# Keys of dilated attention stored in the order of their tokens' residues modulo 4, and a fourth key buffer in place of two slots

## The chip, the core and the metric

The kernel runs on one core of one Trainium2 chip. The metric is the device time of one execution in microseconds; of a kernel with several runs the median is given. Engines are named TensorE (PE, with its weight loads PEld), VectorE (DVE), ScalarE (ACT) and SyncE (SP, which issues all loads and stores here); GpSimd has no part in it.

## What is computed

Two layers work on a sequence of 1024 tokens of width 1024 in float32. In each layer the normalised input is projected to four heads of a gated linear recurrence and to eight attention heads of width 64; both outputs are projected back, and a squared-ReLU layer of width 4096 follows. The attention is causal and has three patterns whose outputs are merged by their softmax denominators: a window of 128 with step 1, of 512 with step 4, of 2048 with step 16.

```python
DILATED_PATTERNS = ((128, 1), (512, 4), (2048, 16))
...
    for window, dilation in DILATED_PATTERNS:
        o, lse = dilated_window_attention(q, k, v, window, dilation)
        outs.append(o)
        lses.append(lse)
    weights = jax.nn.softmax(jnp.stack(lses, axis=0), axis=0)
    o = jnp.einsum('pbhs,pbhsd->bhsd', weights, jnp.stack(outs, axis=0))
```

A key is seen by a query of pattern (window, d) only if both tokens have the same residue modulo d. Steps 4 and 16 both keep the residue modulo 4.

## The kernel before

Every function only records operations (`op`, with engines, an assumed cost, what it reads and writes). `Program.order` then simulates the engines with those costs and writes one fixed order for each engine; `weave` mixes two generators, so that attention stands among projections. Buffers come from pools of the sizes in `COUNT` (line 38): `slot` is a tile of 128 x 512 float32 (71 of them), `kk` one of 128 x 1024 (3), `sc` a bank of PSUM for scores (2). An operation is placed only when its pool has room, so the sizes of the pools change the order too. An engine works strictly in its order; SyncE's order is that of the DMA issues, and an issue that waits holds up those behind it.

Precise products are made of float32r parts: a tile is split in a high and a low part (`split`, `hilo`: a cast on ScalarE, line 323, and a subtraction on VectorE, line 325).

`attn_proj` makes queries and keys of four heads at a time. For j = 1 (keys) the two halves of the rotation come out of two subtractions and additions (lines 828 and 829), are split, and are stored to DRAM buffers kh and kl (line 843), each row of a store being 512 tokens of one feature. Queries (j = 0) are also stored in a second order, q4, by residue modulo 4 (lines 848 to 851).

A head loads its keys, 64 rows of 1024 tokens for each half of the rotation, in two tiles of the pool kk: the high part and the low part (`Head.k`, line 903).

Attention runs in units (head, n) with n from 0 to 5. Units 0 to 3 are near blocks: 128 queries against adjoining keys, widths 128, 256, 384, 512, and four times 256. Units 4 and 5 are far blocks: 128 queries of one residue against the 256 keys of that residue, the slice (x, S, 4) (line 927). `scores` makes a block in two products, one for each part of the keys (line 952), in a bank of PSUM; one instruction of VectorE adds the bias tile tpt, writes the result to SBUF and takes the extreme of each row (line 957). ScalarE takes exponentials (line 968), TensorE transposes (lines 1057 and 1102), the transposed probabilities are split, and products with the values follow (lines 1071 and 1115). Half of the units run beside the second key projection (`attn_proj(1)`), half beside the output projection.

In the squared-ReLU stage `norm_up` puts as many of the four pairs b11 in tiles of the pool kk as that pool has (line 1222); the others take two slots each.

Of the kernel before, what the change touches and what calls it, by code (L numbers as in the profile page):

```python
# [11 lines left out]
F32 = mybir.dt.float32  # L12
# [3 lines left out]
OP = mybir.AluOpType  # L16
# [10 lines left out]
W = 512  # L27
# [7 lines left out]
EARLY = 10  # L35


COUNT = {"kk": 3, "slot": 71, "raw": 4, "trig": 2, "whi": 8, "wlo": 8, "ls": 4, "last": 2, "row": 2, "rc": 4, "z": 2, "gemm": 3, "sc": 2, "tr": 2, "acc": 1,
         "dram": 1 << 20, "const": 1 << 20}
LOOKAHEAD = {"PE": 60e3, "SP": 36e3}  # L40
PATIENCE = 5e3
# [213 lines left out]
def trunk(ctx: ExitStack, tc: tile.TileContext, xT, wts, cols, trig, toep, lmask, ident_d, out):  # L255
# [58 lines left out]
    def whole(b):  # L314
        return b, lambda: b.t
# [261 lines left out]
    for l in range(L):  # L577
# [75 lines left out]
        def hgrn_rec(p, pr):  # L653
            for m in range(2):
                h = 2 * p + m
                last = None
                for hf in range(NH):
# [146 lines left out]
                    hout[h][hf] = keep_  # L804
                    yield

        def attn_proj(u):
            grp = [Group(g0 + 8 + 3 * u + j, f"w{l}a{u}{j}") for j in range(3)]
            q4[u] = Buf(f"q4{l}{u}", "dram", [2, 32, 2, 4, W], F32)
            for hf in range(NH):  # L810
# [7 lines left out]
                for j in range(2):  # L818
# [6 lines left out]
                    tt(whole(t3), whole(pa), whole(sn_), OP.mult)  # L825
                    tt(whole(t2), whole(pb), whole(sn_), OP.mult)
                    tt(whole(t4), whole(pb), whole(cs_), OP.mult)
                    tt(whole(t1), whole(t1), whole(t2), OP.subtract)
                    tt(whole(t3), whole(t3), whole(t4), OP.add)

                    if j == 0:
                        qk_st[0, u, hf] = Buf(f"q{l}{u}{hf}", "dram", [2, 32, 2, 4, W], F32)
# [2 lines left out]
                    for o, t in ((0, t1), (1, t3)):  # L835
                        th, tl = hilo(t, "rt")
                        for part, y in enumerate((th, tl)):
                            if j == 0:
                                d = qk_st[0, u, hf]
                                load(d, lambda d=d, o=o, part=part: d[part, :, o], lambda y=y: y.t.bitcast(F32), 1 << 18, y, True)  # L840
                            else:
                                d = qk_st[1, u][part]
                                load(d, lambda d=d, o=o, hf=hf: d[:, o, :, hf * W:(hf + 1) * W], lambda y=y: y.t.bitcast(F32),
                                     1 << 18, y, True)
                        if j == 0 and hf == 1:
                            for part, y in enumerate((th, tl)):
                                z = slot("rp", F32R)
                                op("ACT", c_act(W), [z], [y], lambda e, z=z, y=y: A.copy(
                                    z.t.rearrange("p (r a) -> p r a", r=4), y.t.bitcast(F32).rearrange("p (a r) -> p r a", r=4)))
                                load(q4[u], lambda d=q4[u], o=o, part=part: d[part, :, o], lambda z=z: z.t.bitcast(F32),  # L850
                                     1 << 18, z, True)
# [89 lines left out]
        def scores(hd, n, st, at):  # L941
# [3 lines left out]
            for i, (q, q0, keys, x0) in enumerate(blocks(hd, n)):  # L945
                w = len(range(*keys.indices(S)))
                if t is None or o + w > W:
                    t, ps, o = slot("sp"), bank("sc", "sc"), 0

                def emit(e, ps=ps, q=q, q0=q0, keys=keys, o=o, w=w):  # L950
                    for part, k in enumerate(k2):
                        PE.matmul(ps[:, o:o + w], lhsT=q[:, q0:q0 + 128], rhs=k[:, keys], start=part == 0, stop=part == 1)  # L952

                op("PE", 2 * c_mm(w), [ps], [q] + k2, emit, join=o > 0)

                def emit(e, ps=ps, t=t, o=o, w=w, m=st.part(at + i), x0=x0):
                    V.tensor_tensor_reduce(t[:, o:o + w], ps[:, o:o + w], tpt[:, x0:x0 + w], -0.125, 3e38,  # L957
                                           OP.add, OP.min, m.t)

                op("DVE", c_tt(w), [t, st.part(at + i)], [ps, tpt], emit, join=True)  # L960
                sp.append((t, o, w))
                o += w
# [613 lines left out]
```

## Time and profile before

| what | value |
|---|---|
| median of 3 runs | 2428.82 us (2427.02 to 2429.88) |
| profiled execution | 2435.95 us |
| its span | 2434.2 us |
| TensorE busy | 2390.8 us (98%) |
| VectorE busy | 1733.8 us (71%) |
| ScalarE busy | 1217.5 us (50%) |
| mean granted clock of TensorE | 0.993 |

The span runs from the first to the last instruction of the profiled execution. Busy times are unions of the recorded instructions. A matmul's recorded length includes the pipeline, so that lengths of neighbours overlap; the pace is the distance between starts. In the waits, "A <- B" says that A stood idle until B was done.

### The profile page before, as it was taken

How to read it: one execution, taken by the hardware profiler on the slowest of the kernel's cores; microseconds unless marked ns; L12 is line 12 of the kernel's file. 1: busy time of each engine (PE TensorE's matmuls, PEld its weight loads, DVE VectorE, ACT ScalarE, POOL GpSimd, SP SyncE). 2: the span in 40 equal slices, each digit the busy share in tenths (PEclk: the TensorE clock that was granted, in tenths of full speed). 3: DMA queues.
4: the chain of work that ended last, by engine and by line, in shares of the span. 5: the costliest groups of instructions: out<-in, count | busy, mean ns of one | idle time of the engine just before them, and what ended most of it. 6: DMA issues, size and time to landing. Idle time of an engine off the chain costs nothing.

```text
span 2434.2 us, 35321 instructions
## 1 busy us (share of the span) xinstructions
PE 2390.8 (98%) x12572; PEld 2029.5 (83%) x12572; DVE 1733.8 (71%) x3414; ACT 1217.5 (50%) x2391; POOL 0.2 (0%) x4
## 2 busy tenths in 40 slices
PE   9999999999999999999999999999999999999998
PEld 7888898887888878888888988898878888888887
DVE  6365877778988667765744668677889885786575
ACT  7233346665744554445532433466656455554453
POOL 0000000000000000000000000000000000000000
PEclk9999999999999999999999999999999999999999
DMA  4011365953455469656420114668344653786562
GB/s 177 27 35 53 130 212 174 272 159 122 160 207 195 152 216 317 222 181 226 169 83 18 62 53 150 209 177 267 120 165 147 225 181 138 261 310 224 182 218 94
DMA packets 189681, 407.19 MB, mean 167 GB/s; under 512 B 22656, under 2 KB 25536, under 8 KB 189504
## 3 DMA queue, kind: packets, MB, share of 16 engines
q1 hardware_dynamic: 189504, 404.93, 49.7%
q8 instruction: 99, 1.62, 0.3%
q14 instruction: 78, 0.64, 0.1%
HBM read 291.37 MB, written 113.48 MB: 166 GB/s over the span
## 4 chain that ended last, share of the span: by engine, by line
PE 91%; DMA 4%; DVE 2%; ACT 2%; SPq 0%; issue 0%; DVEq 0%; ACTq 0%
PE psd L1415 8%; PE psd L1416 8%; PE psd L1417 8%; PE psu L1264 8%; PE psu L1265 8%; PE psu L1266 8%; PE sc L952 2%; PE pa L705 2%; PE pso L383 2%; PE pso L382 2%; PE pso L384 2%; PE pv L1115 1%; PE psv L407 1%; PE psq L382 1%; PE psv L408 1%; PE psv L409 1%
## 5 line engine op out<-in xcount | busy, mean ns | idle before, releaser
L325 DVE TENSOR_TENSOR al<-al,ah 128x512 fp32r<-128x512 f32 x224 | 152.7, 686 | 51.3 <-ACT ah L323 50.7
L323 ACT CAST ah<-al 128x512 fp32r<-128x512 f32 x224 | 137.4, 618 | 97.9 <-DMA al<-a 50.9
L968 ACT ACTIVATE sp<-sp,ls 128x256 f32<-128x256 f32 (+2 forms) x192 | 100.0, 523 | 17.7 <-DVE ls L957 17.3
L957 DVE CUSTOM_DVE_ANT_0 sp<-sc,tpt 128x256 f32<-128x256 f32 (+1 forms) x192 | 83.1, 439 | 35.6 <-PE sc L952 34.0
L952 PE MATMUL sc<-k,hd 128*128 128x256 f32 (+3 forms) x384 | 95.0, 358 | 12.7 <-DMA k<-kl 7.2
L952 PEld LDWEIGHTS sc<-k,hd 128*128 128x128 f32 x384 | 61.2, 195 | 19.6 <-DVE ls L957 6.1
L1247 ACT ACTIVATE c<-c 128x512 f32<-128x512 f32 x96 | 60.5, 630 | 33.2 <-DVE c L312 33.0
L323 ACT CAST pth<-ptr 128x512 fp32r<-128x512 f32 (+1 forms) x96 | 51.3, 552 | 39.5 <-PE ptr L1102 38.1
L1248 ACT ACTIVATE c<-c 128x512 f32<-128x512 f32 x108 | 68.4, 633 | 3.4
L325 DVE TENSOR_TENSOR ptl<-ptr,pth 128x512 fp32r<-128x512 f32 (+1 forms) x96 | 60.7, 641 | 10.9 <-ACT pth L323 9.8
L705 PEld LDWEIGHTS pa<-q,k 128*112 128x112 f32 (+3 forms) x512 | 62.0, 184 | 3.4
L705 PE MATMUL pa<-q,k 128*112 128x64 f32 (+3 forms) x512 | 61.2, 262 | 0.0
L312 DVE TENSOR_TENSOR x<-x,psd 128x512 f32<-128x512 f32 (+1 forms) x68 | 41.8, 652 | 25.3 <-PE psd L1417 25.1
L312 DVE TENSOR_TENSOR x<-x,pso 128x512 f32<-128x512 f32 x64 | 43.4, 681 | 15.2 <-PE pso L384 14.7
L1102 PE MATMUL ptr<-ident,sp 128*128 128x128 f32 x352 | 53.3, 276 | 0.5 <-ACT sp L968 0.4
L1264 PE MATMUL psu<-bt3h,s3h 128*128 128x512 f32 x128 | 50.6, 395 | 3.2 <-ACT u L319 3.2
L1122 ACT COPY pvt<-pv 64x256 f32<-64x256 f32 x80 | 29.6, 370 | 47.0 <-PE pv L1115 45.5
L713 DVE COPY_PREDICATED at<-lmt,pa 126x256 f32<-126x256 uint8 (+1 forms) x64 | 32.8, 512 | 25.1 <-PE pa L705 24.4
L1265 PE MATMUL psu<-bt3l,s3h 128*128 128x512 f32 x128 | 50.3, 393 | 0.0
L1266 PE MATMUL psu<-bt3h,s3l 128*128 128x512 f32 x128 | 50.3, 393 | 0.0
L1265 PE MATMUL psu<-bt1l,s1h 128*128 128x512 f32 x128 | 49.8, 389 | 0.0
L1266 PE MATMUL psu<-b22h,s4l 128*128 128x512 f32 x128 | 49.8, 389 | 0.0
(4980 smaller groups left out, 8136.0 us busy)
## 6 DMA issues: line engine op xcount, KB each, us to landing
al<-a SPq DMA_DIRECT2D x96, 256.0 KB
w0u<-in_wts_dram SPq DMA_DIRECT2D x42, 512.0 KB
w1u<-in_wts_dram SPq DMA_DIRECT2D x42, 512.0 KB
a<-c SPq DMA_DIRECT2D x76, 256.0 KB
al<-a0t SPq DMA_DIRECT2D x64, 256.0 KB
al<-a1t SPq DMA_DIRECT2D x64, 256.0 KB
hd<-q SPq DMA_DIRECT2D x48, 256.0 KB
a0t<-t SPq DMA_DIRECT2D x48, 256.0 KB
```

The source lines that it names most:

```text
L312: lambda e: V.tensor_tensor(dst[1](), a[1](), b[1](), op=kind))
L323: op("ACT", c_act(n), [hi[0]], [src[0]], lambda e: A.copy(hi[1](), src[1]()), join=join)
L325: lambda e: V.tensor_tensor(lo[1](), src[1](), hi[1]().bitcast(F32), op=OP.subtract), join=join)
L705: PE.matmul(pa[0:128 - b, c * 64:c * 64 + 64], lhsT=k[:, c * 128:c * 128 + 128 - b], rhs=by_half(q)[:, c, :, 1, :], start=True, stop=True)
L952: PE.matmul(ps[:, o:o + w], lhsT=q[:, q0:q0 + 128], rhs=k[:, keys], start=part == 0, stop=part == 1)
L968: op("ACT", c_act(w) + 190, [t, sum_], [t, m], lambda e, t=t, o=o, w=w, m=m, sum_=sum_: A.activation(t[:, o:o + w], t[:, o:o + w], AF.Exp, ...
L1264: PE.matmul(ps.t, lhsT=wh[:, cs], rhs=xh.t, start=first and k == 0, stop=False, skip_group_check=True)
L1265: PE.matmul(ps.t, lhsT=wh[:, cs], rhs=xl.t, start=False, stop=False, skip_group_check=True)
L1266: PE.matmul(ps.t, lhsT=wl[:, cs], rhs=xh.t, start=False, stop=k == 3, skip_group_check=True)
L1415: PE.matmul(ps.t, lhsT=wh[:, cs], rhs=th.t[:, ts], start=first and j == 0, stop=False, skip_group_check=True)
L1416: PE.matmul(ps.t, lhsT=wh[:, cs], rhs=tl.t[:, ts], start=False, stop=False, skip_group_check=True)
L1417: PE.matmul(ps.t, lhsT=wl[:, cs], rhs=th.t[:, ts], start=False, stop=j == 15, skip_group_check=True)
```

## The change

Keys are written by the rotation in the order of residue modulo 4 first and position in that residue second, 512 tokens as 4 runs of 128. The store puts each of the four runs where the whole sequence's run of that residue is, so that a stored row has four runs of 256 tokens. Far blocks read 256 adjoining keys; near blocks read four runs, their scores lie by residue in PSUM, and VectorE's instruction of line 957 reads them in the order of tokens while bias and output keep their order. The pool kk has 4 tiles instead of 3, the pool of slots 69 instead of 71, which is the same memory, and `norm_up` now puts all four pairs in kk.

```diff
--- before.py
+++ after.py
@@ -35,7 +35,7 @@
 EARLY = 10
 
 
-COUNT = {"kk": 3, "slot": 71, "raw": 4, "trig": 2, "whi": 8, "wlo": 8, "ls": 4, "last": 2, "row": 2, "rc": 4, "z": 2, "gemm": 3, "sc": 2, "tr": 2, "acc": 1,
+COUNT = {"kk": 4, "slot": 69, "raw": 4, "trig": 2, "whi": 8, "wlo": 8, "ls": 4, "last": 2, "row": 2, "rc": 4, "z": 2, "gemm": 3, "sc": 2, "tr": 2, "acc": 1,
          "dram": 1 << 20, "const": 1 << 20}
 LOOKAHEAD = {"PE": 60e3, "SP": 36e3}
 PATIENCE = 5e3
@@ -804,6 +804,12 @@
                     hout[h][hf] = keep_
                     yield
 
+        def tokens(t):
+            return t, lambda: t.t.rearrange("p (a r) -> p a r", r=4)
+
+        def by_residue(t):
+            return t, lambda: t.t.rearrange("p (r a) -> p a r", r=4)
+
         def attn_proj(u):
             grp = [Group(g0 + 8 + 3 * u + j, f"w{l}a{u}{j}") for j in range(3)]
             q4[u] = Buf(f"q4{l}{u}", "dram", [2, 32, 2, 4, W], F32)
@@ -825,8 +831,14 @@
                     tt(whole(t3), whole(pa), whole(sn_), OP.mult)
                     tt(whole(t2), whole(pb), whole(sn_), OP.mult)
                     tt(whole(t4), whole(pb), whole(cs_), OP.mult)
-                    tt(whole(t1), whole(t1), whole(t2), OP.subtract)
-                    tt(whole(t3), whole(t3), whole(t4), OP.add)
+                    if j == 0:
+                        tt(whole(t1), whole(t1), whole(t2), OP.subtract)
+                        tt(whole(t3), whole(t3), whole(t4), OP.add)
+                    else:
+                        k1, k3 = slot("kp"), slot("kp")
+                        tt(by_residue(k1), tokens(t1), tokens(t2), OP.subtract)
+                        tt(by_residue(k3), tokens(t3), tokens(t4), OP.add)
+                        t1, t3 = k1, k3
 
                     if j == 0:
                         qk_st[0, u, hf] = Buf(f"q{l}{u}{hf}", "dram", [2, 32, 2, 4, W], F32)
@@ -840,8 +852,9 @@
                                 load(d, lambda d=d, o=o, part=part: d[part, :, o], lambda y=y: y.t.bitcast(F32), 1 << 18, y, True)
                             else:
                                 d = qk_st[1, u][part]
-                                load(d, lambda d=d, o=o, hf=hf: d[:, o, :, hf * W:(hf + 1) * W], lambda y=y: y.t.bitcast(F32),
-                                     1 << 18, y, True)
+                                load(d, lambda d=d, o=o, hf=hf: d.t.rearrange("i o h (r a) -> i o h r a", r=4)[
+                                    :, o, :, :, hf * 128:hf * 128 + 128], lambda y=y: y.t.bitcast(F32).rearrange(
+                                        "p (r a) -> p r a", r=4), 1 << 18, y, True)
                         if j == 0 and hf == 1:
                             for part, y in enumerate((th, tl)):
                                 z = slot("rp", F32R)
@@ -949,13 +962,21 @@
 
                 def emit(e, ps=ps, q=q, q0=q0, keys=keys, o=o, w=w):
                     for part, k in enumerate(k2):
-                        PE.matmul(ps[:, o:o + w], lhsT=q[:, q0:q0 + 128], rhs=k[:, keys], start=part == 0, stop=part == 1)
+                        dst, src = ps[:, o:o + w], k.t.rearrange("p (r a) -> p r a", r=4)
+                        if keys.step:
+                            src = src[:, keys.start]
+                        else:
+                            src = src[:, :, keys.start // 4:keys.stop // 4]
+                        PE.matmul(dst, lhsT=q[:, q0:q0 + 128], rhs=src, start=part == 0, stop=part == 1)
 
                 op("PE", 2 * c_mm(w), [ps], [q] + k2, emit, join=o > 0)
 
-                def emit(e, ps=ps, t=t, o=o, w=w, m=st.part(at + i), x0=x0):
-                    V.tensor_tensor_reduce(t[:, o:o + w], ps[:, o:o + w], tpt[:, x0:x0 + w], -0.125, 3e38,
-                                           OP.add, OP.min, m.t)
+                def emit(e, ps=ps, t=t, o=o, w=w, m=st.part(at + i), x0=x0, step=keys.step):
+                    s, dst, bias = ps[:, o:o + w], t[:, o:o + w], tpt[:, x0:x0 + w]
+                    if not step:
+                        s = s.rearrange("p (r a) -> p a r", r=4)
+                        dst, bias = (x.rearrange("p (a r) -> p a r", r=4) for x in (dst, bias))
+                    V.tensor_tensor_reduce(dst, s, bias, -0.125, 3e38, OP.add, OP.min, m.t)
 
                 op("DVE", c_tt(w), [t, st.part(at + i)], [ps, tpt], emit, join=True)
                 sp.append((t, o, w))
```

Where instructions move: on SyncE, at the second head of the first layer; kh and kl are the stored parts of keys, k a head's tile. Before:

```order
L344 DMA k<-kh_2398 64x1024 x2
L344 DMA hd<-q_2272 128x512
L344 DMA hd<-q_2590 128x512
L344 DMA mh_3_1_0_3366<-mhh 128x512
L344 DMA mh_3_1_1_3373<-mhl 128x512
L344 DMA hd<-q_2597 128x512
L344 DMA q_3406<-rth 32x4x512 x2
L344 DMA q_3406<-rtl 32x4x512 x2
L344 DMA hd<-q_2272 128x512
L344 DMA k<-kl_2412 64x1024 x2
L344 DMA trig<-in_trig_dram 128x512 x2
```

Now:

```order
L344 DMA k<-kh_2400 64x1024 x2
L344 DMA k<-kl_2414 64x1024 x2
L344 DMA hd<-q_2272 128x512
L344 DMA mh_3_1_0_3376<-mhh 128x512
L344 DMA mh_3_1_1_3390<-mhl 128x512
L344 DMA hd<-q_2592 128x512
L344 DMA hd<-q_2599 128x512
L344 DMA q_3413<-rth 32x4x512 x2
L344 DMA q_3413<-rtl 32x4x512 x2
L344 DMA hd<-q_2272 128x512
L344 DMA k<-kh_2400 64x1024
L344 DMA trig<-in_trig_dram 128x512 x2
```

The load of the low part has moved from behind the loads of queries and the stores to right behind that of the high part; where it stood, the third head's high part begins.

On VectorE, at the rotation of the first keys (t are the rotation's products, kp the new tiles, rth and rtl the parts). Before:

```order
L312 TENSOR_TENSOR t_2363<-psb,trig 128x512
L312 TENSOR_TENSOR t_2369<-psb,trig 128x512
L312 TENSOR_TENSOR t_2311<-t_2311,t_2363 128x512
L312 TENSOR_TENSOR t_2313<-t_2313,t_2369 128x512
L312 TENSOR_TENSOR q<-q,tot 128x4x64
L325 TENSOR_TENSOR rtl<-t_2311,rth 128x512
L325 TENSOR_TENSOR rtl<-t_2313,rth 128x512
```

Now:

```order
L312 TENSOR_TENSOR t_2363<-psb,trig 128x512
L312 TENSOR_TENSOR t_2369<-psb,trig 128x512
L312 TENSOR_TENSOR kp<-t_2311,t_2363 128x128x4
L312 TENSOR_TENSOR kp<-t_2313,t_2369 128x128x4
L312 TENSOR_TENSOR q<-q,tot 128x4x64
L325 TENSOR_TENSOR rtl<-kp,rth 128x512 x2
```

The two last steps of the rotation write four-run tiles of their own instead of writing over an input; what follows keeps its place.

On TensorE, at the end of the first head and the start of the second (line 1102 before is 1123 now, 952 is 970, 1057 is 1078). Before:

```order
L1071 MATMUL pv<-pp,v_3202 128x256
L1071 MATMUL pv<-pp,v_3282 128x256
L1071 MATMUL pv<-pp,v_3211 128x256
L1071 MATMUL pv<-pp,v_3286 128x256
L975 MATMUL lt<-ident,ls 32x128
L952 MATMUL sc<-k,hd 128x128 x2
L952 MATMUL sc<-k,hd 128x384 x2
```

Now:

```order
L1123 MATMUL ptr<-ident,sp 128x128 x4
L970 MATMUL sc<-k,hd 128x256 x2
L970 MATMUL sc<-k,hd 128x128 x2
L382 MATMUL psa<-n_1h,w0a111h 128x512
L383 MATMUL psa<-n_1l,w0a111h 128x512
L384 MATMUL psa<-n_1h,w0a111l 128x512
L382 MATMUL psa<-n_1h,w0a111h 128x512
```

The second head's first score product, 128 columns, stood behind the first head's last value products and now stands among the products of the key projection some 25 rows earlier.

## Rows read from the trace of the kernel before

**Rows 1.** the page, busy us, share of the span and instructions of each engine
```profile
PE 2390.8 (98%) x12572; PEld 2029.5 (83%) x12572; DVE 1733.8 (71%) x3414; ACT 1217.5 (50%) x2391; POOL 0.2 (0%) x4
```

**Rows 2.** stretches: length, PE, PEld, DVE, ACT, POOL busy (count), clock, DMA share, GB/s
```profile
330.00:550.00 220.00, 211.28 (x1319) 187.45 (x1317) 166.39 (x444) 137.59 (x378) 0.00 (x0) 0.99 0.68 206
1534.00:1755.00 221.00, 213.15 (x1321) 188.74 (x1320) 166.67 (x445) 137.82 (x380) 0.00 (x0) 0.98 0.67 205
380.00:430.00 50.00, 49.04 (x334) 45.02 (x333) 40.88 (x109) 34.56 (x91) 0.00 (x0) 1.00 0.57 170
```

**Rows 3.** timeline, TensorE, far products: start us, length, line, operation, tiles, shapes, count
```profile
1598.74 1.09 PE L952 MATMUL sc<-k,hd 128*128 128x256 f32 x4
1599.65 0.42 PE L382 MATMUL psa<-n_1h,w1a111h 128*128 128x512 f32 x1
...
1601.48 0.70 PE L952 MATMUL sc<-k,hd 128*128 128x256 f32 x2
1601.99 0.44 PE L382 MATMUL psa<-n_1h,w1a111h 128*128 128x512 f32 x1
```

**Rows 4.** timeline, TensorE, near products of a later head
```profile
1614.42 0.40 PE L952 MATMUL sc<-k,hd 128*128 128x256 f32 x2
1614.66 0.28 PE L407 MATMUL psva<-w1a121h,n_0h 128*128 128x256 f32 x1
```

**Rows 5.** waits of TensorE, whole run: who for whom, us, times, longest
```profile
PE sc L952 <- DMA k<-kl: 7.2, 7, 2.2
PE pv L1115 <- DVE ar L1124: 4.7, 8, 1.0
PE sc L952 <- DVE ls L957: 4.5, 4, 2.5
```

**Rows 6.** timeline, SyncE's queue, loads and stores around the second head's keys
```profile
368.16 1.12 SPq L344 DMA_DIRECT2D k<-kl  x2
369.38 1.00 SPq L344 DMA_DIRECT2D trig<-in_trig_dram  x2
370.48 0.57 SPq L344 DMA_DIRECT2D kh<-rth  x1
...
373.60 1.33 SPq L344 DMA_DIRECT2D k<-kh  x2
```

**Rows 7.** timeline, TensorE, two waits for the low part of keys
```profile
372.55 0.22 PE L952 MATMUL sc<-k,hd 128*128 128x128 f32 x1
374.04 0.71 PE L952 MATMUL sc<-k,hd 128*128 128x128 f32 x3 [1.26 <-DMA k<-kl]
...
497.28 0.33 PE L952 MATMUL sc<-k,hd 128*128 128x128 f32 x1 [1.89 <-DMA k<-kl]
```

**Rows 8.** stretches after two such waits, granted clock third from the end
```profile
498.40:501.80 3.40, 3.40 (x15) 3.14 (x14) 1.21 (x3) 0.00 (x0) 0.00 (x0) 0.50 1.03 242
1580.40:1583.80 3.40, 3.40 (x13) 2.82 (x12) 1.91 (x8) 2.26 (x8) 0.00 (x0) 0.50 1.05 281
```

**Rows 9.** VectorE by line and shape: count, busy us, mean ns, idle before
```profile
L957 DVE CUSTOM_DVE_ANT_0 sp<-sc,tpt 128x256 f32<-128x256 f32 x144 | 59.2, 416 | 28.6 <-PE sc L952 27.8
L957 DVE CUSTOM_DVE_ANT_0 sp<-sc,tpt 128x128 f32<-128x128 f32 x16 | 4.6, 288 | 4.2 <-PE sc L952 4.1
L687 DVE COPY_PREDICATED at<-lmt,pa 128x128 f32<-128x128 uint8 x32 | 14.1, 441 | 0.3
L312 DVE TENSOR_TENSOR ar<-ar,rb 128x512 f32<-128x512 f32 x24 | 16.5, 685 | 0.8 <-DMA rb<-l 0.4
L312 DVE TENSOR_TENSOR rb<-rb,ar 128x512 f32<-128x512 f32 x4 | 4.3, 1072 | 1.4 <-DMA rb<-l 1.4
```

**Rows 10.** the page, the DMA queue of loads and stores: packets, MB, share
```profile
q1 hardware_dynamic: 189504, 404.93, 49.7%
```

**Rows 11.** waits of all engines, VectorE's for scores
```profile
DVE sp L957 <- PE sc L952: 34.0, 45, 3.5
```

## The prediction

> **What bounds the kernel now.** I read the busy shares first. TensorE is busy for 2390.8 of 2434.2 us [rows 1], so whatever shortens its own work is paid back almost in full, and work of another engine counts only where TensorE waits for it. Then the stretches: the change touches the two attention stages (330 to 550 us and 1534 to 1755 us) and the key projections just before and in them. In the two stages together TensorE is busy 424.4 of 441 us, so it idles 16.6 us, and VectorE is busy 333.1 us, 76% [rows 2]. Third, the timeline of TensorE, for the pace of one score product (a matmul's length overlaps the next one, so the pace is read from start to start). Four products against every fourth key, 256 columns each, run from 1598.74 to 1599.65: 0.228 us each [rows 3]. Two products of the same 256 columns against adjoining keys run from 1614.42 to 1614.66: 0.12 us each [rows 4]. Shape, types and weights are alike; only the step between the keys that are read differs. Last, what TensorE waits for: in the whole run 7.2 us, in 7 waits, for the low part of a head's keys to land, which is the largest entry; then 4.7 us for the sums of attention values and 4.5 us for VectorE to take a bank of scores [rows 5].
>
> **Part 1, far score products (patterns that step by 4).** Per head 4 blocks times 2 parts of the keys; 16 heads in the two layers: 128 products. Their keys become adjoining, and 0.228 becomes 0.12 us: 128 x 0.108 = 13.8 us. Where such a group stands behind transposes it is a little slower still (0.51 us for the two at 1601.48) [rows 3], 0.255 - 0.12 = 0.135 each, and 128 x 0.135 = 17.3 is the other end. I take 14.5, near the group of four, which stands among ordinary work. All of it is TensorE's own time.
>
> **Part 2, near score products.** Their keys are now read as 4 runs of a quarter of the width, 32 to 128 adjoining keys. No row shows a read with three jumps in it. A jump at every key costs 0.108 us for 256 of them, 0.4 ns each; three jumps in each of 256 products would be 0.3 us in all. I take 0; the other end, every near product as slow per column as a far one, is rival 4.
>
> **Part 3, VectorE reads the near scores in another order.** The bank now holds the scores by residue, and the instruction that adds the bias steps by a quarter of the width at every element, to put them back in the order of tokens. Columns: 128 + 256 + 384 + 512 + 4 x 256 = 2304 a head, 36,864 in all; the 64 far instructions stay as they are. No row shows such a read of a PSUM bank by this instruction. The nearest row is the product of two tiles in SBUF, one read at a step of 128 elements: 1072 ns for 512 elements where the same work in order takes 685 [rows 9], 0.756 ns more for each. By that row: 36,864 x 0.756 = 27.9 us of VectorE, the near 256-column instruction going from 416 to about 610 ns. Lower end 0 (a stepped read cannot be quicker than 416 ns, which is already a column a cycle beside the 288 of 128 columns: 1.0 ns each). Upper end, the masked copy that writes every second element, 441 ns for 128 against 288 [rows 9]: 1.2 ns each, 44 us. I take 27.9.
> By the Trainium skill (PSUM — Partial Sum Buffer, Specifications (TRN2)) PSUM has lines of 8 bytes, and a non-contiguous pattern slows matmuls significantly; it gives no figure for VectorE, and no run here shows one. If it holds for VectorE's reads, every element of these fetches a line of its own, which speaks for a price at least like that of the SBUF row and for rival 3.
>
> What hides it: in the two stages VectorE has 441 - 333 = 108 us free. After the change it has 333 + 28 + 3 (part 4) = 364 us of work beside 424 - 14.5 = 410 us of TensorE's, 89%. A stretch that already runs so, 380 to 430 us, has VectorE at 40.9 of 50 us, 82%, with TensorE idle for only 0.96 us [rows 2]: a high share alone doesn't stop TensorE. But the score banks are two, so a longer read gives a bank back later, by 0.19 us for 256 columns and 0.39 for 512; behind it on VectorE stand the low parts of the transposed probabilities, for which the value products wait. TensorE's two waits on VectorE, 4.7 + 4.5 = 9.2 us now, grow; I let them grow by half, +5 us. Ends: 0 (all covered) and +28 (all on the path).
>
> **Part 4, the keys' rotation writes by residue.** 16 instructions of 512 elements that now write at a step of 128: by the same row 16 x 0.387 = 6.2 us of VectorE, half of it in the attention stages, half in the stage before, where it stands under products of the projection. On the path 0; if the cover were gone, 6. Two more slots are held for a moment, and the pool has two fewer; no slot wait is among TensorE's large entries [rows 5], so 0, with 3 us as the price if the shorter pool delays a load or a transpose now and then.
>
> **Part 5, stores of the keys in runs of 512 bytes.** 32 stores, 128 rows each, three more packets a row: 12,288 more. The queue's mean packet takes 49.7% x 2434 x 16 / 189,504 = 0.102 us [rows 10]; if each added one took as long (they are a fourth of the size), a group of four stores would take 1536 x 0.102 / 16 = 9.8 us more of the transfer engines; if time goes by bytes, 0. Such a group stands on SyncE's queue right behind the loads of trigonometric tables at 369 us, and keys of the next head are the loads behind it. I take 0 on the path, because with part 6 these keys are wanted a head later, some 27 us; without that cover a part of the 9.8 would stand in front of a head, in four places.
>
> **Part 6, the fourth buffer.** With three, a head's high part is loaded early, and its low part only when the head before has done its last far product: issued at 368.16 [rows 6], wanted at 372.6, arrived at 374.04, 1.26 us late; at 497.28 it is 1.89 us late [rows 7]. With four, both parts stand together on SyncE's queue, a head ahead, so the 7.2 us of [rows 5] go. After the two longest of these waits the granted clock is 0.5, its lower level, for 3.4 us (498.4 and 1580.4) [rows 8]; at half pace 1.7 us are lost each time, 3.4 in both. What is late next: the transfers are not idle (share 0.68 and 0.67 in the stages [rows 2]), so the value loads or a merge's small transfers may end a wait that is covered by the key wait today. Ends: -10.6 and 0. I take -8.
>
> **Sum.** -14.5 - 8 + 5 = -17.5 us. The profiled execution took 2435.95 us, 1.75 around its span; it would take 2418.5. The median of the runs is 2428.82, 7.1 below the profiled one, and the terms are absolute, so 2428.8 - 17.5 = 2411.3; I write 2412.
>
> **Rivals.**
> 1. The forecast, with VectorE's price near the SBUF row: 2412, by the terms' usual spread 2403 to 2421. Chance 0.55.
> 2. Stepped reads of PSUM are free: VectorE gets no longer (but for part 4) and the +5 goes, 2407. For it: nothing in the trace shows a stepped PSUM read. Against it: 1072 against 685 in SBUF. Chance 0.14. The Trainium skill (VectorE: DVE Perf Modes, Mode 1× (REGULAR) — the baseline) says that the plain mode makes no assumption on strides or PSUM operands and gives a result a cycle; by that rule this rival would hold, but the SBUF row, at nearly 2 ns an element, does not agree with it.
> 3. VectorE becomes the bound, and the kernel is slower. Place: the near scores in both stages. It decides from (410 - 333 - 3) / 36,864 = 2.0 ns more an element, nearly three times the SBUF row. At 3.0 ns VectorE has 333 + 3 + 111 = 447 us of work, already above today's 441 for the stages with no idle time; VectorE's present waits for scores, 34 us [rows 11], don't all go, and with a third of them left the stages take 458: 2428.8 + 17 = 2446. For it: the unknown price in PSUM. Against it: both measured prices of stepping are 0.76 and 1.2. Chance 0.10.
> 4. The change doesn't do what it says: the slow pace of far products isn't the step of the keys, or four-run reads are as slow. Then part 1 gives nothing, and -8 + 5 remain: 2426. Against it: 0.12 beside 0.228 with nothing else different. Chance 0.07.
> 5. Waits come back: part 1 holds, but the queues are written for a VectorE that keeps up, the waits on it double (+10), and the keys' 8 us turn up as waits for values or for the merge: 2428.8 - 14.5 + 10 = 2424. For it: TensorE already waits for the sums of values. Chance 0.14.
>
> **How the numbers follow.** A measurement of this kernel can tell some 0.2%, 4.9 us, from no change: faster is below 2424, slower above 2433.7. Faster: cases 1, 2 and half of 5, 0.76; slower: case 3, 0.10; the same: case 4 and the other half of 5, 0.14. The range: low end, all of parts 1 and 6 at their better ends with no price in part 3, 2428.8 - 17.3 - 10.6 = 2401; high end 2426, which takes in case 5 and leaves out case 3 and part of case 4.
>
> **What would show it.** Far products at 0.12 us from start to start; near ones unchanged. The bias instruction of 256 columns in two groups, 416 ns for far and about 610 for near; the rotation's two at about 1.07 us. No wait of TensorE for keys, and no clock at 0.5 near the start of a head. TensorE's waits for VectorE at 12 to 16 us instead of 9. The forecast is wrong if near products slow down, if the bias instruction takes over 0.9 us for 256 columns, or if TensorE's idle time in the stages grows above today's 16.6 us.

## The result, and the profile after

The changed kernel takes 2409.42 us (median of 4 runs, 2408.74 to 2411.52) beside 2427.92 for the kernel before on the same chip (4 runs, 2420.86 to 2429.88): ratio 0.9923 [0.991, 0.9935], 18.5 us less. The forecast was 2412, 2401 to 2426. The profiled run took 2409.73 us, of which 2407.9 are the span. The profile of before was taken from a run of 2435.95 us, some 7 above its median, so differences between these two profiles are too large by about as much; a second profile of before, below, corrects for that.

The page after, busy us, share of the span and instructions, and then its row on the DMA queue (packets, MB, share of 16 engines' span):

```profile
PE 2370.5 (98%) x12572; PEld 2014.9 (84%) x12572; DVE 1734.8 (72%) x3414; ACT 1216.5 (51%) x2391; POOL 0.2 (0%) x4
...
q1 hardware_dynamic: 201792, 404.93, 50.3%
```

TensorE is busy 20.3 us less than in [rows 1] with the same 12,572 instructions; a part of that is chance, since the stretches at the lower clock sum to 36.6 us in that profile and 21.0 in this one, and the means of several profiles, below, give 16.3. VectorE, which was to get longer by 34 us, is busy 1.0 us more. The queue has the 12,288 packets more that the prediction counted on top of [rows 10], and its share rose by 0.6 points.

TensorE's timeline, far products (start, length, line, operation, count), with the instruction behind each group:

```profile
1582.40 0.65 PE L970 MATMUL sc<-k,hd 128*128 128x256 f32 x4
1582.88 0.44 PE L382 MATMUL psa<-n_1h,w1a111h 128*128 128x512 f32 x1
...
1600.27 0.40 PE L970 MATMUL sc<-k,hd 128*128 128x256 f32 x2
1600.51 0.28 PE L407 MATMUL psva<-w1a120h,n_0h 128*128 128x256 f32 x1
```

The four far products take 0.48 us from their start to the start of the next instruction, 0.12 each, where [rows 3] has 0.228. The two near ones in the last pair of lines, now read in four runs, take 0.24, as in [rows 4].

VectorE by form (line, operation, shapes, count | busy us, mean ns | idle before and its releaser):

```profile
L979 DVE CUSTOM_DVE_ANT_0 sp<-sc,tpt 128x256 f32<-128x256 f32 x144 | 58.4, 415 | 23.3 <-PE sc L970 22.3 <-issue 0.2
...
L312 DVE TENSOR_TENSOR kp<-t,t 128x512 f32<-128x512 f32 x16 | 17.1, 1086 | 0.0
...
L979 DVE CUSTOM_DVE_ANT_0 sp<-sc,tpt 128x512 f32<-128x512 f32 x16 | 10.9, 681 | 0.1
```

and the last of them in the kernel before:

```profile
L957 DVE CUSTOM_DVE_ANT_0 sp<-sc,tpt 128x512 f32<-128x512 f32 x16 | 11.0, 684 | 2.3 <-PE sc L952 2.1
```

Line 979 is the 957 of [rows 9]. Its 144 instructions of 256 columns, 80 of which now step through PSUM, take 415 ns where all took 416, and the widest ones, all stepped, take 681 where they took 684. A stepped read of PSUM costs VectorE nothing here. The rotation's write to `kp`, stepped in SBUF, takes 1086 ns, as the prediction priced it from 1072.

What TensorE waits for, whole run (us, times, longest):

```profile
PE pso L382 <- ACT ma_0h L323: 4.9, 2, 2.5
PE sc L970 <- DVE ls L979: 4.9, 10, 1.1
PE ptr L1123 <- ACT sp L989: 4.2, 4, 1.8
PE sc L970 <- DMA hd<-q: 3.0, 3, 1.8
...
PE pv L1136 <- DVE ar L1145: 0.6, 2, 0.3
```

No wait for keys is left of the 7.2 us of [rows 5], and the wait of the value products for the attention sums fell with it, from 4.7 to 0.6. In their place stand waits of score products for queries (`hd`), 3.0 us, and of transposes for ScalarE's exponentials, 4.2. Only the second comes in every profile: the three runs below that keep this order of instructions and fast far products wait for queries 0.3 us or not at all, and for exponentials 6.0 to 7.6.

SyncE's queue, where [rows 6] has the low part of the keys late:

```profile
345.23 1.09 SPq L344 DMA_DIRECT2D k<-kh  x2
346.37 1.24 SPq L344 DMA_DIRECT2D k<-kl  x2
```

Both parts are asked for together, at 345 us, for the second head, whose first score products run at 368.30.

The attention stages, and the stretch behind one of the new waits (length, PE, PEld, DVE, ACT, POOL busy, granted clock, DMA share, GB/s):

```profile
331.00:541.00 210.00, 203.59 (x1327) 181.75 (x1326) 168.28 (x450) 139.34 (x381) 0.00 (x0) 1.00 0.70 216
1520.00:1731.00 211.00, 204.17 (x1326) 182.64 (x1325) 168.58 (x450) 138.78 (x381) 0.00 (x0) 0.99 0.70 215
...
1661.90:1665.30 3.40, 3.40 (x13) 2.88 (x11) 1.25 (x3) 0.71 (x2) 0.00 (x0) 0.50 1.06 339
```

The stages' 441 us of [rows 2] are 421 now, and TensorE's idle time in them went from 16.6 to 13.2 us. The last line shows that the clock still falls: behind a wait of 1.84 us for queries, at 1661.02, the granted clock is 0.50 for 3.4 us, the lower of its two levels (1.2 of 2.4 GHz), while TensorE is busy throughout.

### The profile page after: what moved, and what is told of

Read it like the earlier page. It is cut to its first block, busy times and chain, and to the rows that moved or that the text cites. A ratio compares the mean times of both kernels' runs of the same rounds, so it can differ in the third digit from the quotient of the medians.

```text
span 2407.9 us, 35355 instructions
## 1 busy us (share of the span) xinstructions
PE 2370.5 (98%) x12572; PEld 2014.9 (84%) x12572; DVE 1734.8 (72%) x3414; ACT 1216.5 (51%) x2391; POOL 0.2 (0%) x4
## 4 chain that ended last, share of the span: by engine, by line
PE 91%; DMA 3%; DVE 2%; ACT 2%; issue 1%; SPq 0%; DVEq 0%; ACTq 0%
PE psd L1438 8%; PE psd L1437 8%; PE psd L1436 8%; PE psu L1285 8%; PE psu L1287 8%; PE psu L1286 8%; PE pso L383 2%; PE pso L384 2%; PE pso L382 2%; PE pa L705 2%; PE pv L1136 2%; PE sc L970 2%; PE ptr L1123 1%; PE psv L407 1%; PE psq L382 1%; PE psv L408 1%
## 5 line engine op out<-in xcount | busy, mean ns | idle before, releaser
L970 PE MATMUL sc<-k,hd 128*128 128x256 f32 (+3 forms) x384 | 80.5, 313 | 8.0 <-DVE ls L979 4.9
L1287 PE MATMUL psu<-bt1h,s1l 128*128 128x512 f32 x128 | 49.8, 389 | 0.0
```

Source lines behind the costliest of these rows:

```text
L970: PE.matmul(dst, lhsT=q[:, q0:q0 + 128], rhs=src, start=part == 0, stop=part == 1)
L1287: PE.matmul(ps.t, lhsT=wl[:, cs], rhs=xh.t, start=False, stop=k == 3, skip_group_check=True)
```

## Experiments

The experiments ask four things: what each half of the change is worth alone, where the difference between the far products' 14.5 us and the end went, whether the stepped reads and writes cost anything, and whether a version is faster still. Each was timed against the kernel before on its own chip. A kernel below that reads wrong keys issues the same work.

**The order alone.** Against the changed kernel:

```diff
-COUNT = {"kk": 4, "slot": 69, ...
+COUNT = {"kk": 3, "slot": 71, ...
```

> The change without the fourth key buffer (three key tiles, 71 slots). Theory A, the forecast's terms: far products at 0.12 us instead of 0.228 give 14.5 us by themselves, the waits for the low part of keys (7.2 us and two stretches at the lower clock) stay; so 14 to 15 us under the kernel before, and some 4 us over the whole change. Theory B, the gain comes mostly from the other order that the planner writes once both parts of the keys are loaded together: 0 to 6 us under the kernel before. Of part 5: the stores in runs of 512 bytes stand in front of keys that are wanted at once here; if they cost, the waits for keys grow above 7.2 us.

Measured: 2426.18 beside 2429.6, ratio 0.9989 [0.9979, 0.9999], 2.7 us less. The far products run at the fast pace (its score products are busy 80.6 us in all), yet most of that doesn't reach the end. The figure lies in theory B's range and not in theory A's.

**The fourth buffer alone.** The same line edited the other way in the kernel before.

```diff
-COUNT = {"kk": 3, "slot": 71, ...
+COUNT = {"kk": 4, "slot": 69, ...
```

> The kernel before with four key tiles and 69 slots, keys in the order of tokens. Theory A: the key waits of 7.2 us go, and far products stay at 0.228 us; 4 to 8 us under the kernel before, and the two alone add up to the 18.5 us of the change. Theory B: the order makes the gain, so this alone gives 12 us or more. A third outcome, that the waits come back elsewhere: within 3 us of the kernel before.

Measured: 2416.21, ratio 0.9947 [0.9932, 0.9961], 12.9 us less (9.5 to 16.5). What TensorE waits for then:

```profile
PE ptr L1102 <- ACT sp L968: 5.1, 5, 3.1
PE pso L382 <- ACT ma_0h L323: 4.9, 2, 2.5
PE sc L952 <- DVE ls L957: 3.0, 4, 1.1
PE sc L952 <- DMA hd<-q: 1.6, 1, 1.6
```

The wait for keys is gone by the buffer alone, and so are the 4.7 us for the sums, while 5.1 us for exponentials have come. Here too the time is theory B's, 12 us or more: what the buffer gives is more than the waits for keys.

**Far products at the old pace in the changed kernel.** Everything else stays; the far products read every fourth column of a tile that is ordered by residue, so their scores belong to wrong keys.

```diff
-                            src = src[:, keys.start]
+                            src = k[:, keys.start::4]
```

> The whole change, its order of instructions untouched, but far products read every fourth column of the key tile again (so other keys than they should: the scores of the far blocks are of wrong keys). Theory A: pace back at 0.228 to 0.24 us, TensorE's busy time up by 14 to 15 us, and the time 14 us over the change, about 2423 us. Theory B, or a pace that has another cause than the step: within 4 us of the change.

Measured: 2420.3, ratio 0.9963 [0.995, 0.9976]; the changed kernel's ratio is 0.0040 lower, 9.7 us, and the intervals don't overlap. TensorE's timeline shows the old pace:

```profile
1587.90 1.09 PE L970 MATMUL sc<-k,hd 128*128 128x256 f32 x4
1588.81 0.42 PE L382 MATMUL psa<-n_1h,w1a111h 128*128 128x512 f32 x1
```

0.91 us for four, 0.228 each, the figure of [rows 3]. So the step causes the slow pace. The group of all score products (busy us, mean ns), in this kernel:

```profile
L970 PE MATMUL sc<-k,hd 128*128 128x256 f32 (+3 forms) x384 | 94.2, 354 | 3.6 <-DVE ls L979 3.3
```

and in the changed kernel:

```profile
L970 PE MATMUL sc<-k,hd 128*128 128x256 f32 (+3 forms) x384 | 80.5, 313 | 8.0 <-DVE ls L979 4.9
```

In the kernel before:

```profile
L952 PE MATMUL sc<-k,hd 128*128 128x256 f32 (+3 forms) x384 | 95.0, 358 | 12.7 <-DMA k<-kl 7.2 <-DVE ls L957 4.5 <-DMA hd<-q 0.6
```

13.7 us of the products' own time for 9.7 at the end; the idle time in front of them is 4.4 us longer where they are fast. The intervals of the two ratios together are wider than the 4 us between these figures. The waits for exponentials are there at the old pace as well, so the faster products didn't bring them:

```profile
PE ptr L1123 <- ACT sp L989: 6.2, 4, 3.6
```

**Near products and VectorE in plain order.** Near products read adjoining columns (wrong keys), VectorE reads without steps.

```diff
-                            src = src[:, :, keys.start // 4:keys.stop // 4]
+                            src = k[:, keys]
...
-                    if not step:
+                    if False:
```

> The whole change with near products reading adjoining columns of the key tile and VectorE reading their scores in the order in which they lie (the near scores are of wrong keys); order of instructions untouched. As forecast, a stepped read costs VectorE 0.756 ns an element and the path 5 us: then this kernel is 3 to 6 us faster than the change. By the trace after, where the bias instruction of 256 columns takes 415 ns as before: no difference within 2 us, neither for the read of four runs by TensorE nor for the stepped read by VectorE.

Measured: 2409.6, ratio 0.9917 [0.9902, 0.9932]: the changed kernel's time. Its 256-column bias instructions take 415 ns as well, all of them without steps:

```profile
L979 DVE CUSTOM_DVE_ANT_0 sp<-sc,tpt 128x256 f32<-128x256 f32 x144 | 58.4, 415 | 23.1 <-PE sc L970 21.8 <-issue 0.5
```

Neither the four runs nor the stepped PSUM reads show a cost, in the instructions or, within the intervals, at the end.

**Stores in long rows.** With three buffers and with four, the keys' stores go back to runs of 2048 bytes (the stored keys then lie in a wrong order).

```diff
-                                load(d, lambda d=d, o=o, hf=hf: d.t.rearrange("i o h (r a) -> i o h r a", r=4)[
-                                    :, o, :, :, hf * 128:hf * 128 + 128], ...
+                                load(d, lambda d=d, o=o, hf=hf: d[:, o, :, hf * W:(hf + 1) * W], ...
```

> The key order without the fourth buffer (as the first experiment, 2426.2 us), with its stores in one run of 2048 bytes a row again (the halves of the sequence then stand one behind the other, so products read other keys than they should). The first experiment gave 3.4 us where TensorE's busy time fell by 14.5. Theory C, the stores of 512-byte runs take the rest, because they stand in front of the loads of keys that are wanted at once: some 8 to 11 us faster, near 2416. Theory D, the rest is lost to waits for the keys themselves and to the lower clock behind them, which come with three buffers whatever the stores do: within 3 us of 2426.

> The whole change with stores in one run of 2048 bytes a row (products read other keys than they should). The forecast put the 512-byte runs at 0 on the path with the fourth buffer: within 2 us of the change, 2409. If the runs cost something even so: 3 us or more faster.

Measured: with three buffers 2427.24, 0.9995 [0.9984, 1.0005], where short runs gave 0.9989; with four 2410.61, 0.9925 [0.9909, 0.994], where they gave 0.9923. The theory that the short runs delay the keys, and so eat the gain of the order with three buffers, fell.

**Two second profiles.** The kernel before, and the order alone, once more; nothing is edited.

> The kernel before, unchanged, for a second profile, since its first profiled execution was 6 to 7 us over the median. Theory D: the idle time and the stretches at the lower clock differ between executions, so this one has less of both, 28 to 33 us idle and 4 to 7 stretches; TensorE's busy time apart from the clock the same, 2385 to 2391.

> The first experiment, unchanged, for a second profile, since its first was 4 us under its median. Theory D: TensorE busy 2376 again, and more idle time than 33.8 us, or more stretches at the lower clock than 6, most of it at the loads of a head's low part; theory C: waits for keys of the fifth head, whose stores are just before, above all.

Waits of TensorE in the kernel before, from 2424.42 us:

```profile
PE pv L1115 <- DVE ar L1124: 4.7, 8, 1.0
PE sc L952 <- DMA k<-kl: 4.4, 7, 1.6
PE sc L952 <- DVE ls L957: 3.5, 4, 1.9
```

and in the order alone, from 2425.53 us:

```profile
PE sc L970 <- DMA k<-kl: 7.6, 8, 2.1
PE pv L1136 <- DVE ar L1145: 5.4, 8, 1.6
PE sc L970 <- DVE ls L979: 3.9, 4, 2.4
...
PE ptr L1123 <- ACT sp L989: 2.5, 7, 0.7
```

The key waits of one kernel differ between two profiles (7.2 in [rows 5], 4.4 here), so a single pair could not tell. The ten profiles of the four kinds together tell more. The table has the means of TensorE's busy time and of the span's rest, us, from the pages (the kernels with old far pace, plain near order and long stores stand with their kind):

| buffers, far pace | profiles | busy | rest of the span | span |
|---|---|---|---|---|
| three, slow | 2 (before) | 2388.6 | 39.8 | 2428.4 |
| three, fast | 3 | 2377.6 | 47.2 | 2424.8 |
| four, slow | 2 | 2384.1 | 33.0 | 2417.1 |
| four, fast | 3 (the change) | 2372.3 | 36.2 | 2408.5 |

Down the table one reads: with three buffers the fast pace takes 11.0 us off TensorE's work and gives 7.4 back in the rest of the span. The waits for keys are 7.2 and 4.4 us at the slow pace and 8.7, 11.0 and 7.6 at the fast one, those of transposes for exponentials up to 0.4 and then 1.6 to 2.5. With four buffers it takes 11.8 off and gives 3.2 back. The rest of the span differs much between profiles of one kind, though: 43.4 and 36.2 with three buffers at the slow pace, 43.8, 50.9 and 47.0 at the fast one; with four buffers the five lie between 32.3 and 37.4. The buffer takes 6.8 us of the rest at the slow pace and 11.0 at the fast one, and 4.5 to 5.3 of busy time.

**What a step costs each engine.** A kernel of probes alone, 114.12 us, which computes nothing of the reference: 24 products of 256 columns in each order of reading, and 8 VectorE additions and 8 ScalarE copies of 512 elements for each order in PSUM and in SBUF.

```diff
+    reads = {"one": lambda: kr.t[:, 0:256], "two": lambda: by(2)[:, 0:256, 0], "three": lambda: kr.t[:, 0:768:3],
+             "four": lambda: by(4)[:, :, 0], "pairs": lambda: by(8)[:, :, 0:2], "fours": lambda: by(8)[:, 0:64, 0:4],
+             "runs": lambda: kr.t.rearrange("p (r a) -> p r a", r=4)[:, :, 64:128]}
```

> Only probes, none of the layers. TensorE: groups of 24 products of 256 columns whose keys are read adjoining (one), every second, third and fourth column (two, three, four), as pairs with a gap of six, as fours with a gap of four, as four runs of 64. If the slow pace comes from a jump at every key alone, whatever its length: two, three and four at 0.23 us, pairs and fours at 0.12 to 0.18, runs at 0.12. If it comes from fetching a new stretch of 16 bytes for every key: two at 0.12, three about 0.17, four 0.23, pairs 0.12. VectorE and ScalarE: 512 elements from a bank of PSUM (ps) and from SBUF (sb), in order (line), hopping by 128 (hop), by 4 (quad) and by 2 (duo), and one that writes in hops (dout). By the traces so far: from PSUM 0.68 us in any order on VectorE; from SBUF 0.68 in order and about 1.08 hopping; writing in hops 1.09. Of ScalarE only the reading at a step of 4 from SBUF is known, 1.13 against 0.62; if PSUM is free of that too, 0.6 there.

TensorE's timeline; a group's pace is the distance to the next start over 24:

```profile
6.91 3.13 PE L565 MATMUL peone<-k,wr 128*128 128x256 f32 x24 [1.00 <-ACT k L550]
9.88 5.60 PE L565 MATMUL petwo<-k,wr 128*128 128x256 f32 x24
15.30 5.62 PE L565 MATMUL pethree<-k,wr 128*128 128x256 f32 x24
20.74 5.78 PE L565 MATMUL pefour<-k,wr 128*128 128x256 f32 x24
26.34 5.78 PE L565 MATMUL pepairs<-k,wr 128*128 128x256 f32 x24
31.94 3.01 PE L565 MATMUL pefours<-k,wr 128*128 128x256 f32 x24
34.79 3.03 PE L565 MATMUL peruns<-k,wr 128*128 128x256 f32 x24
37.65 3.04 PE L565 MATMUL peone<-k,wr 128*128 128x256 f32 x24
```

Adjoining columns take 0.12 us a product, every second, third or fourth column 0.23, pairs with a gap of six 0.23; groups of four with a gap of four 0.12, and four runs of 64 0.12. The last line begins a second round of all seven, whose figures are the same to 0.004 us, and the granted clock is 1.00 throughout.

VectorE and ScalarE (`ps` in a name is a read of PSUM, `sb` of SBUF; `line` in order, `duo` a step of 2, `quad` of 4, `hop` of 128; `dout` writes by hops):

```profile
L594 ACT COPY csbquad<-sb 128x512 f32<-128x512 f32 x8 | 9.3, 1158 | 0.2
...
L589 DVE TENSOR_TENSOR dsbquad<-sb,other 128x512 f32<-128x512 f32 x8 | 8.9, 1112 | 0.2
L589 DVE TENSOR_TENSOR dsbhop<-sb,other 128x512 f32<-128x512 f32 x8 | 8.9, 1107 | 0.2
L602 DVE TENSOR_TENSOR dout<-sb,other 128x512 f32<-128x512 f32 x8 | 8.8, 1098 | 0.2
...
L589 DVE TENSOR_TENSOR dsbline<-sb,other 128x512 f32<-128x512 f32 x8 | 5.5, 693 | 0.3
...
L589 DVE TENSOR_TENSOR dpsline<-peruns,other 128x512 f32<-128x512 f32 x8 | 5.5, 691 | 22.9 <-PE peruns L565 22.6
L589 DVE TENSOR_TENSOR dsbduo<-sb,other 128x512 f32<-128x512 f32 x8 | 5.5, 691 | 0.2
L589 DVE TENSOR_TENSOR dpshop<-peruns,other 128x512 f32<-128x512 f32 x8 | 5.5, 691 | 10.1 <-ACT cpshop L594 9.8
L589 DVE TENSOR_TENSOR dpsquad<-peruns,other 128x512 f32<-128x512 f32 x8 | 5.5, 691 | 5.2 <-ACT cpsquad L594 5.0
L594 ACT COPY csbduo<-sb 128x512 f32<-128x512 f32 x8 | 5.5, 682 | 0.2
L594 ACT COPY csbline<-sb 128x512 f32<-128x512 f32 x8 | 5.0, 620 | 0.2
...
L594 ACT COPY cpsquad<-peruns 128x512 f32<-128x512 f32 x8 | 4.7, 586 | 6.1 <-DVE dpshop L589 5.8
```

In SBUF a hop takes VectorE 1.6 times as long as the plain order, in PSUM no longer; ScalarE likewise, 586 ns in PSUM by fours and 1158 in SBUF.

**The rotation written in order.** The changed kernel without the stepped write; the keys stay in the order of tokens in the tile, so what is read by residue is wrong.

```diff
-                        tt(by_residue(k1), tokens(t1), tokens(t2), OP.subtract)
-                        tt(by_residue(k3), tokens(t3), tokens(t4), OP.add)
+                        tt(whole(k1), whole(t1), whole(t2), OP.subtract)
+                        tt(whole(k3), whole(t3), whole(t4), OP.add)
```

> The whole change with the two last steps of the keys' rotation written in the order of tokens (in the same extra tiles; keys then stand in another order than products take them for). The forecast priced the 6.2 us of VectorE at 0 on the path: within 2 us of the change. The kernel with far products stepped (2420.3) is 4 us slower than the fourth buffer alone (2416.2) though TensorE's score products cost the same in both; if the rotation's stepped writes are the reason, this one is 3 to 4 us faster than the change.

Measured: 2406.47, ratio 0.991 [0.9896, 0.9925], its `kp` at 681 ns. That is 3.2 us below the change by the ratios, but the intervals overlap: whether the stepped write costs nothing or up to the 6.5 us that it takes of VectorE (16 x 0.405) is not settled.

**The order made by the split.** The rotation writes in place as before, in order; the two instructions that split keys into high and low parts read by steps and write by runs instead.

```diff
-                        th, tl = hilo(t, "rt")
+                        if j == 0:
+                            th, tl = hilo(t, "rt")
+                        else:
+                            th, tl = slot("rth", F32R), slot("rtl", F32R)
+                            split(runs(th), runs(tl), (t, lambda t=t: t.t.rearrange("p (a r) -> p r a", r=4)))
```

> The whole change with the order of the keys made a step later: the rotation writes in place in the order of tokens, and the split into parts reads it by residue, on ScalarE 0.5 us more in each of 16 casts, on VectorE 0.4 us more in each of 16 subtractions, and no extra tiles. If the extra tiles or VectorE's place before ScalarE cost the change something: 2 to 4 us faster than it. If nothing of the ordering is on the path: within 2 us.

Measured: 2412.46, ratio 0.9943 [0.9929, 0.9957], some 5 us slower than the change by the ratios, with intervals that overlap a little, and not 2 to 4 faster. Two instructions step now where one did: over queries and keys the high part takes 875 ns on ScalarE and the low 883 on VectorE in the mean.

**A fifth buffer.**

```diff
-COUNT = {"kk": 4, "slot": 69, ...
+COUNT = {"kk": 5, "slot": 67, ...
```

> The whole change with five key tiles and 67 slots. No wait for keys is left with four, so the forecast's view is no gain: within 2 us, or a little slower if two slots fewer hold something up. If the gain of the fourth buffer came from the rearranged orders rather than from the waits, another rearrangement could move it by 4 us or more either way.

Measured: 2412.69, ratio 0.9934 [0.9922, 0.9946], no better than the change; its 2.7 us more by the ratios are within the intervals. With four no wait for keys was left to take. So of the two versions that could stand in the change's place neither beats it.

## Why the prediction was right, and where not

The sign, the time (2412 for 2409.42) and the two sources were right; two terms were off by 4 to 5 us each and cancel, so the closeness of the time is in part luck. It is also as near to rival 2's 2407 as to the forecast. Forecast: far pace -14.5, given back +5, buffer -8, the rest of the order 0, in all -17.5. Measured: far pace with what it gives back -9.7, buffer alone -12.9, in all -22.6; the change is -18.7 by its ratio, so the rest of the order costs some 4. The same 4 stand between two kernels timed side by side, 2420.3 with far products at the old pace and 2416.21 with the buffer alone; but their intervals overlap and the spans of their two profiles differ by 1.0 us, so the figure could also be near 0.

**Part 1 (-14.5).** The step is the cause, and the size is right for TensorE: the group of score products is busy 95.0 us in the profile of before and 80.5 after. The end moved by 9.7, so by these figures 4 to 5 came back, which is about as much as the noise; the table's means show 3.2 as time in which TensorE is not busy.

**Part 2 (0).** Right: 0.12 us a near product in the trace, no time that shows in the run with near products in plain order, and 0.12 in the probe of four runs.

**Part 3 (+27.9 us of VectorE, +5 on the path).** This step failed. It took the price of a stepped read of SBUF for one of PSUM, because no nearer row was there. The SBUF price itself is right (1107 ns beside 693), the PSUM price is nothing (691 beside 691, and 415 ns with and without the steps). Rival 2 had that mechanism, at 0.14, with 2407. The row for the upper end was no price of a step alone either: it set a masked copy beside the bias instruction, which is another operation. By the Trainium skill (VectorE: DVE Perf Modes, Mode 1× (REGULAR) — the baseline) the plain mode gives a result a cycle and makes no assumption on strides or PSUM operands; the runs agree for PSUM, 691 ns in any order, and in SBUF at a step of 2, but not at steps of 4 and more there. The 8-byte lines that the Trainium skill gives PSUM (PSUM — Partial Sum Buffer, Specifications (TRN2)), which the prediction weighed as a reason for a high price, show no effect on VectorE's or ScalarE's reads here. The +5 was still the size of what came back (4 to 5), and that is luck, since the longer reads that it was worked out from are not there. Rival 5 had returned and grown waits, 18 us of them, of which about a quarter came. Which they are with four buffers is not shown: of the large waits only that of score products for VectorE to free their bank is longer at the fast pace in every profile (4.9, 3.8 and 4.6 us beside 3.0 and 3.3).

**Part 4 (6.2 us of VectorE, 0 on the path).** The price is right, 1086 ns for an estimated 1072. That it is wholly hidden is doubtful: without the stepped write the time was 3.2 us lower, within the intervals, and that would be most of the 4 us that the rest of the order seems to cost. This stays open.

**Part 5 (0).** Right: 12,288 packets more, and no time that shows from taking them away, with three buffers or four.

**Part 6 (-8).** Half of the mechanism is right, and the size was off: -12.9 alone. The working had 7.2 us of waits and 3.4 of clock, -10.6, and took -8 for what would be late next. What came next was more than that deduction: 5.1 and 6.2 us for exponentials in the two profiles with four buffers at the slow pace, where 0.4 and less stood before. The step that failed is that it put at nothing the other waits which the fourth buffer removes, above all the sums' 4.7 us. Those don't seem to hang on how late the keys are: they are 4.7 us in 8 waits in both profiles of before, whose waits for keys are 7.2 and 4.4. That speaks for the other order of instructions that is written for four buffers, theory B of the first two experiments; no run has that order without the buffer.

The table has 6.8 us of idle time and some 5 of busy time in place of the 8. The stretches at the lower clock, 0.50 granted, sum in the mean of each kind to 33.1 us (three buffers, slow pace), 33.9 (three, fast), 27.7 (four, slow) and 28.1 (four, fast): some 5.6 us fewer with four buffers, which at half pace is an estimated 2.8 of the 5, near the working's 3.4. The rest of the busy time stays open, and single profiles reach from 21.0, that of the change, to 42.1. The other thing that a fourth buffer changes, `norm_up`, gives about 1 us a layer at most: from the first product of the second layer's squared-ReLU stage to the end TensorE takes 624.5 and 624.7 us with four buffers at the slow pace and 627.1 and 626.5 before, and 1.4 us of that are six products of the output projection that now stand in front of it.

**What the parts do to each other.** No part of the sum had this. With three buffers the order is worth 2.7 us, with four the step from 0.9947 to 0.9923, 5.8. The intervals of the two steps are wider than their difference. The table points the same way, with late keys more of a faster product comes back as waits, but its profiles scatter by as much. That the buffer also makes room for the order's gain is likely, then, and not shown.

The bounds held: rivals 3 (VectorE the bound) and 4 (the step not the cause) are excluded by 415 ns and by 0.12 us. The idle time in the stages, 13.2 us, stayed under the 16.6 above which the forecast would have been wrong.

## What to carry to other kernels

Lay out what TensorE streams so that it comes in runs of at least four fp32 elements (runs of one and two were slow, three was not tried), and put the reordering that this needs into VectorE's or ScalarE's read of PSUM, which was free here, and not into a read or write of SBUF. A faster product on the bound engine can be worth much less at the end than on the engine: here 2.7 of 11.0 us with the keys late. So measure it together with the buffer that removes the wait, and alone; and a size of a pool that a planner reads changes its whole order, so look at all waits and not only at those of the tile that the pool holds. Compare several profiles of each kernel before a wait of a few microseconds is put down to a change: the same kernel's key waits were 7.2 and 4.4 us.

## What the runs showed of the hardware

TensorE's reads of fp32r columns fall to half the pace already at a step of 2 (0.226 us for 256 columns beside 0.12), and pairs with a gap are as slow (0.233); of the probes with gaps only those with runs of four or more, 16 bytes, are at full pace (0.119). A step of 2, 3 or 4 costs nearly the same.

By the Trainium skill (SBUF — State Buffer, Specifications (TRN2)) SBUF has lines of 16 bytes and wants two hits in each for full bandwidth. VectorE agrees with it, 691 ns at a step of 2 beside 693 in order and 1112 at a step of 4; TensorE does not, since pairs, two hits in a line, run at half pace.

ScalarE pays 682 ns at a step of 2 beside 620 in order and 1158 at a step of 4 in SBUF, and 586 in every order from PSUM.
